# Down-projection of a gated MLP on one core: where the sums of weight quarters are made, how many raw tiles the ring holds, and beside which up-projection pairs the steps stand

## The chip, the core and the metric

The program runs on one core of a Trainium2 chip. The metric is the device time of one execution in microseconds (us), taken as the median of several. A core has TensorE (PE; its weight loads are listed as PEld), VectorE (DVE), ScalarE (ACT), GpSimd (POOL) and SyncE (SP, which here only issues transfers). They run beside each other and wait for each other by semaphores; 16 DMA engines move data between HBM and the core's SBUF. The clock that TensorE is granted has two levels, 1.2 and 2.4 GHz; the profile gives it as a share of the full one.

## The reference, cut to what matters

One layer of a hybrid decoder for 512 tokens of width 1024. Two token mixers come first (some 60% of the time, untouched). The change is in the conv-gated MLP and in the gated input embedding behind it:

```python
h = rms_norm(x, ffn_norm[i])
act, lin = jnp.split(h @ w_ffn_up[i], 2, axis=-1)            # 1024 -> 2 x 2816
act = causal_dwconv(act, w_ffn_conv[i]) + b_ffn_conv[i]
x = x + (jax.nn.gelu(act) * lin) @ w_ffn_down[i]             # 2816 -> 1024
g = jax.nn.sigmoid(rms_norm(x, ple_norm[i]) @ w_ple_gate[i])
x = x + g * (p[i] @ w_ple_proj[i])
return rms_norm(x, final_norm)
```

## The kernel before

Every product is made of three matmuls on float32r parts (high times high, high times low, low times high). A weight block is loaded as it is into a raw tile of a ring in SBUF (tag `raw`; in this part of the program four tiles of 8 KB per partition). `wsplit` then makes the high part on ScalarE (`whi`, L164) and the low part on VectorE (`wlo`, L165), 128x1024 numbers at a time; there are four buffers of each. A raw tile comes free when its last `wlo` is made, and only then can the transfer for the tile that takes its place start.

`up(j)`, j from 0 to 10, makes one pair of hidden blocks: 4 column blocks of 24 matmuls each (lines L169 to L171, output `pa`), then the convolution, the GELU and the product, on ScalarE and VectorE, into a tile `g2`. `combine` (L293 to L302) makes from each such tile the operands `ch` and `cl` of the down-projection.

The down-projection is a block algorithm of seven steps in place of eight products (`strassen`, table `STEPS`). It runs in three quarters called 1 to 3 here (`down(0)`, `down(1)`, `down(2)`): the first two have four row blocks (`kh` 4, 24 matmuls in a step), the last three (18 matmuls). Lines L333 to L335 are its matmuls, with the PSUM banks `sX`, `sZ` and `sY`; L1070 adds a finished bank to the residual x2. Each step needs one weight tile, which is a quarter of the block (1 MB; 0.75 MB in the last), or the sum of two, three or four quarters: step 0 "11", step 1 "11"+"12", step 2 "11"+"12"+"22", step 3 "22", step 4 "21", step 5 "12"+"22", step 6 all four. The sums are made by transfers: the first quarter is loaded from SP's queue, and each further one is added to what lies in the tile by an accumulating transfer that GpSimd issues, each of them after the one before has landed:

```python
if i == 0:
    nc.sync.dma_start(raw, blk)
else:
    nc.gpsimd.dma_start(raw, blk, accum_op=ALU.add)
```

Pairs and steps alternate: three steps behind pair 4, three behind pair 5 and one behind pair 6, and the same behind pairs 8, 9 and 10; quarter 3 runs its seven steps without a pair between. `over(q)` then combines the pairs that were ready before their quarter had its turn. In quarter 3, `add` also starts the norm of each token tile that is complete (`x3n0` to `x3n3`: square on ScalarE, a small chain on GpSimd, scaling on VectorE, transposes on TensorE into h3). Two products follow: p with w_ple_proj (`pb` with operand pTh, in two halves of 24 matmuls) and h3 with w_ple_gate (`pb` with operand h3h).

The instructions of an engine run in the order in which the program lists them. That order, and the slots of tiles, were set by a scheduler when the program was built; `with ahead()` puts weight loads and splits as early as their buffers allow.

Of the kernel before, what the change touches and what calls it, by code (L numbers as in the profile page):

```python
# [14 lines left out]
P = 128  # L15
# [28 lines left out]
def tile_hybrid_block(  # L44
# [244 lines left out]
    def combine(pool, g2, ch, cl, j):  # L289
# [14 lines left out]
            op0=ALU.mult, op1=ALU.subtract,  # L304
        )

    def strassen(src, ch, cl, kh, add):

        v = src.rearrange("(k two p) n -> two p k n", two=2, p=P)
        banks = {}
        for n, (c, parts, b, th, h, sign) in enumerate(STEPS):
            with ahead():
                raw = rp[0].tile([P, kh, 512], F32, tag="raw", name=f"raw{uid()}", bufs=rp[1])
                for i, q in enumerate(parts):
                    blk = v[int(q[0]) - 1][:, :, 512 * int(q[1]) - 512 : 512 * int(q[1])]
                    if i == 0:
                        nc.sync.dma_start(raw, blk)
                    else:  # L320
                        nc.gpsimd.dma_start(raw, blk, accum_op=ALU.add)  # L321
                ws = [wsplit(raw[:, k : min(k + 2, kh), :], min(2, kh - k), 512) for k in range(0, kh, 2)]
            new = b not in banks
            if new:
                banks[b] = [sm_ps(f"s{b}{uid()}") for _ in range(2)]
            for t in range(2):
                ps = banks[b][t]
                tok = slice(t * P, (t + 1) * P)
                for k in range(kh):
                    hi, lo = ws[k // 2]  # L330
                    a_h, a_l = ch[:, c, k, tok], cl[:, c, k, tok]

                    TE.matmul(ps, lhsT=a_h, rhs=hi[:, k % 2, :], start=new and k == 0, stop=False, skip_group_check=True)  # L333
# [10 lines left out]
    class Norm:  # L344


        def __init__(self, pool, xt, name, tag="xn", bufs=4):
            self.x = [xt[:, :512], xt[:, 512:]]
            self.name = name
            self.xn = [pool.tile([P, 512], F32, tag=tag, name=f"{name}_{h}", bufs=bufs) for h in range(2)]  # L350
            self.ss = cp.tile([P, 4], F32, tag="ss", name=name + "s", bufs=4)
            self.rs = cp.tile([P, 1], F32, tag="rs", name=name + "r", bufs=4)
            self.n = 0
# [69 lines left out]
    with tc.tile_pool(name="xin", bufs=1, reuse_waits="tile") as xin:  # L423
        with ahead(200000):
            xts = [xin.tile([P, D], F32, name=f"xt{t}") for t in range(NT)]
            raw0 = [rp[0].tile([P, KD, 2 * P], F32, tag="raw", name=f"raw0_{i}", bufs=rp[1]) for i in range(2)]

            def load_x(t):
                nc.sync.dma_start(xts[t], x[t * P : (t + 1) * P, :])

            def load_w(i):
                nc.sync.dma_start(
                    raw0[i // 2][:, :, i % 2 * P : (i % 2 + 1) * P], srcs0[i].rearrange("(k p) n -> p k n", p=P)
                )

            load_x(0)
            g1 = gain_bc(xin, "g1", mixer_norm)
            load_x(1)
            load_w(0)
            load_x(2)  # L440
            load_w(1)
            load_x(3)
            load_w(2)
            load_w(3)
            nms = [Norm(xin, xts[t], f"xn{t}") for t in range(NT)]

            def sq(t):
                nms[t].square(0)
                nms[t].gather()
                nms[t].square(1, eng=V if t < 2 else None)  # L450

            def w0(i, eng=V):
                return wsplit(raw0[i // 2][:, :, i % 2 * P : (i % 2 + 1) * P], KD, P, eng=eng)

            sq(0)
            sq(1)
            norm_T(nms[0], g1, hT, 0)
            ws0 = [w0(0, G)]
            norm_T(nms[1], g1, hT, 1)
            for t in (2, 3):  # L460
                sq(t)
                ws0.append(w0(t - 1))
                for h in range(2):
                    nms[t].gained(g1, h)
                nms[t].rstd()
                for h in range(2):
                    transpose_split(nms[t].scaled_gained(h, V), hT, t, h, nms[t].name + "T")
            ws0.append(w0(3))
# [523 lines left out]
    for t in range(NT):  # L992
        nc.scalar.dma_start(x2[t], x[t * P : (t + 1) * P, :])
    lnp = ctx.enter_context(tc.tile_pool(name="lnp", bufs=1, side="right", reuse_waits="tile"))
    g2 = gain_bc(lnp, "g2", ffn_norm)
    h2 = new_hT("h2")

    def residual(nm, h, after=None):
        cols = slice(h * 512, (h + 1) * 512)

        def emit(t, ps):
            V.tensor_tensor(x2[t][:, cols], x2[t][:, cols], ps, op=ALU.add)
            if h == 1:
# [16 lines left out]

    rx.close()
    fx = ExitStack()
    rp[:] = fx.enter_context(tc.tile_pool(name="rp2", bufs=1, reuse_waits="tile")), 4
    fax = ExitStack()
    cmp = fax.enter_context(tc.tile_pool(name="cmp", bufs=1, reuse_waits="tile"))
    ch = cmp.tile([P, 7, 4, 256], R, name="ch")
# [37 lines left out]
    def down(q):  # L1064
        kh = min(4, KF // 2 - 4 * q)
        last = 4 * q + kh == KF // 2

        def add(t, h, ps, sign, n):
            xs = x2[t][:, h * 512 : (h + 1) * 512]
            V.tensor_tensor(xs, xs, ps, op=ALU.add if sign > 0 else ALU.subtract)  # L1070
            if not last:
                return

            if n in (3, 5):
                nms[t] = Norm(lnp, x2[t], f"x3n{t}")
                nms[t].square(1)
                nms[t].gather()
            elif n in (4, 6):
                nms[t].square(0)
                norm_T(nms[t], g3, h3, t)  # L1080

        return strassen(w_ffn_down[1024 * q : 1024 * q + 256 * kh, :], ch, cl, kh, add)
# [13 lines left out]
    for j in range(4):  # L1096
        up(j)
    d = down(0)
    for j, n in ((4, 3), (5, 3), (6, 1)):
        up(j)  # L1100
        run(d, n)
    over(0)
    up(7)
    g3 = gain_bc(lnp, "g3", ple_norm)
    d = down(1)
    for j, n in ((8, 3), (9, 3), (10, 1)):
        up(j)
        run(d, n)
    over(1)
    h3 = new_hT("h3")  # L1110

    def quad(name, dt=F32):
        return cmp.tile([P, 2, T], dt, tag="g2", name=name, bufs=5)


    pt = quad("pt").rearrange("p a (t d) -> p (a t) d", t=2)
    nc.sync.dma_start(pt, p.rearrange("(t q) d -> q t d", q=P))
    pTh, pTl = quad("pTh", R), quad("pTl", R)
    for k in range(2):
        ps = sm_ps(f"pT{k}")  # L1120
        for t in range(NT):
            TE.transpose(ps[:, t * P : (t + 1) * P], pt[:, t, k * P : (k + 1) * P], ident)
        S.copy(pTh[:, k, :], ps)
        V.tensor_tensor(pTl[:, k, :], ps, f32(pTh[:, k, :]), op=ALU.subtract)
    run(down(2), 7)

    pjs = [rp[0].tile([P, 4, 512], F32, tag="raw", name=f"pj{i}", bufs=rp[1]) for i in range(2)]
    pj = [[pjs[t // 2][:, 2 * (t % 2) + h, :] for h in range(2)] for t in range(NT)]
    for h in range(2):
        cols = slice(h * 512, (h + 1) * 512)  # L1130
        proj_b(w_ple_proj[:, cols], (pTh, pTl), 2, lambda t, ps: S.copy(pj[t][h], ps))
    fax.close()
    gtp = fx.enter_context(tc.tile_pool(name="gtp", bufs=1, reuse_waits="tile"))

# [6 lines left out]
    def add_gated(t, h, a, b, ps):  # L1141
        s = piece(f"psig{h}_{t}_{a}")[:, a:b]
        xs = x2[t][:, 512 * h + a : 512 * h + b]
        S.activation(s, ps, AF.Sigmoid)
        V.tensor_tensor(s, s, pj[t][h][:, a:b], op=ALU.mult)
        V.tensor_tensor(xs, xs, s, op=ALU.add)
        if h == 0:
            fin[t] = Norm(gtp, x2[t], f"on{t}", "g", 24)
        fin[t].square(h, a, b)
        if (h, b) != (1, 512):  # L1150
            fin[t].gather()
        if h == 0:
# [70 lines left out]
```

## Time and profile before

| | us |
|---|---|
| median of 3 runs | 1210.12 (1208.36 to 1212.64) |
| the profiled execution | 1207.67 |
| its span, from the first to the last instruction | 1205.9 |
| mean granted TensorE clock over the span | 0.988 |

The span is the trace's own length; the execution is 1.77 us longer. Times of rows count from the start of the span. A matmul's duration in a row is modelled and overlaps the next one's, so the pace of TensorE is read from the distance of starts. In a timeline row the bracket gives the engine's idle time just ahead of it and what ended that.

### The profile page before, as it was taken

The numbers are of one execution on the slowest core, as the hardware profiler recorded it, in microseconds if no ns is written. First come the engines' busy times: TensorE is split into PE (matmuls) and PEld (weight loads), VectorE is DVE, ScalarE is ACT, GpSimd is POOL, SyncE is SP. The second block draws the span as 40 slices with busy tenths as digits, with TensorE's granted clock in tenths as the row PEclk, the third lists the DMA queues.
The fourth block names the chain that finished last, engine by engine and source line by source line (L and its number), as shares of the span: only waits on it lengthen the run. The fifth ranks groups of instructions, "written<-read, shape, count | busy, mean of one in ns | idle before, by whom it ended". The sixth has DMA issues, their size and how long they took to land.

```text
span 1205.9 us, 14072 instructions
## 1 busy us (share of the span) xinstructions
PE 1161.5 (96%) x5540; PEld 958.6 (79%) x5540; DVE 665.8 (55%) x864; ACT 518.7 (43%) x850; POOL 160.6 (13%) x178
## 2 busy tenths in 40 slices
PE   6999999999999999999999999999999999988696
PEld 6887887888887778888888888988888788866485
DVE  5867657676667356342333344665556556537455
ACT  4666483662572155443432322544343343424443
POOL 7004023040031000000111000000000010012202
PEclk9999999999999999999999999999999999989898
DMA  7332123222231253223143335434776696698431
GB/s 204 105 105 71 35 71 95 80 71 70 73 91 47 70 175 105 71 70 101 46 115 82 94 105 140 119 109 123 161 205 167 148 214 178 155 203 193 103 123 70
DMA packets 160370, 137.59 MB, mean 114 GB/s; under 512 B 5792, under 2 KB 125216, under 8 KB 160304
## 3 DMA queue, kind: packets, MB, share of 16 engines
q1 hardware_dynamic: 149536, 114.41, 32.4%
q0 software_dynamic: 10192, 20.19, 9.7%
q10 hardware_dynamic: 576, 2.10, 0.5%
q8 instruction: 43, 0.70, 0.2%
q14 instruction: 23, 0.19, 0.0%
HBM read 134.58 MB, written 2.10 MB: 113 GB/s over the span
## 4 chain that ended last, share of the span: by engine, by line
PE 84%; DMA 6%; DVE 4%; issue 2%; ACT 2%; POOL 1%; SPq 1%; POOLq 0%; ACTq 0%; DVEq 0%
PE pa L170 16%; PE pa L169 16%; PE pa L171 16%; PE pb L249 7%; PE pb L251 7%; PE pb L250 7%; DMA raw<-in_w_ffn_down_dram 5%; PE yd L608 2%; PE sX L333 1%; PE sX L334 1%; PE sX L335 1%; PE st L616 1%; DVE wlo L165 1%; PE yo L605 1%; DMA raw<-in_w_in_dram 1%
## 5 line engine op out<-in xcount | busy, mean ns | idle before, releaser
L165 DVE TENSOR_TENSOR wlo<-raw,whi 128x1024 fp32r<-128x1024 f32 x208 | 255.6, 1234 | 305.3 <-ACT whi L164 305.0
L164 ACT CAST whi<-raw 128x1024 fp32r<-128x1024 f32 (+2 forms) x209 | 216.1, 1039 | 390.6 <-PE pa L170 205.3
L169 PE MATMUL pa<-h1h,whi 128*128 128x512 f32 (+1 forms) x416 | 159.4, 383 | 0.2 <-ACT h1h L403 0.2
L171 PE MATMUL pa<-h1h,wlo 128*128 128x512 f32 (+1 forms) x416 | 157.3, 378 | 0.0
L170 PE MATMUL pa<-h1l,whi 128*128 128x512 f32 (+1 forms) x416 | 156.6, 377 | 0.1
L169 PE MATMUL pa<-h2h,whi 128*128 128x512 f32 (+1 forms) x384 | 142.7, 372 | 0.0
L170 PE MATMUL pa<-h2l,whi 128*128 128x512 f32 (+1 forms) x384 | 142.6, 372 | 0.0
L171 PE MATMUL pa<-h2h,wlo 128*128 128x512 f32 (+1 forms) x384 | 142.6, 372 | 0.0
L249 PE MATMUL pb<-whi,h1h 128*128 128x512 f32 x256 | 99.7, 394 | 0.8 <-DVE accb L668 0.8
L250 PE MATMUL pb<-wlo,h1h 128*128 128x512 f32 x256 | 99.8, 390 | 0.0
L251 PE MATMUL pb<-whi,h1l 128*128 128x512 f32 x256 | 99.4, 392 | 0.0
L169 PEld LDWEIGHTS pa<-h1h,whi 128*128 128x128 f32 x416 | 79.2, 190 | 14.9 <-issue 0.7
L170 PEld LDWEIGHTS pa<-h1l,whi 128*128 128x128 f32 x416 | 79.1, 190 | 14.4 <-issue 0.7
L171 PEld LDWEIGHTS pa<-h1h,wlo 128*128 128x128 f32 x416 | 79.0, 190 | 13.9 <-issue 0.2
L171 PEld LDWEIGHTS pa<-h2h,wlo 128*128 128x128 f32 x384 | 72.4, 188 | 12.5
L169 PEld LDWEIGHTS pa<-h2h,whi 128*128 128x128 f32 x384 | 72.3, 188 | 12.5
L170 PEld LDWEIGHTS pa<-h2l,whi 128*128 128x128 f32 x384 | 72.4, 188 | 12.4
L321 POOL DMA_DIRECT2D raw<-in_w_ffn_down_dram x21 | 27.2, 1373 | 330.0 <-DVE wlo L165 184.6
L249 PEld LDWEIGHTS pb<-whi,h1h 128*128 128x128 f32 x256 | 48.1, 188 | 10.5 <-DVE accb L668 1.2
L251 PEld LDWEIGHTS pb<-whi,h1l 128*128 128x128 f32 x256 | 48.1, 188 | 9.8
L250 PEld LDWEIGHTS pb<-wlo,h1h 128*128 128x128 f32 x256 | 48.1, 188 | 9.3
L533 DVE SCALAR_TENSOR_TENSOR acc<-pa,prm,acc 128x511 f32<-128x511 f32 (+2 forms) x72 | 52.6, 742 | 2.9 <-ACT acc L531 2.0
(376 smaller groups left out, 2011.1 us busy)
## 6 DMA issues: line engine op xcount, KB each, us to landing
raw<-in_w_in_dram SPq DMA_DIRECT2D x48, 512.0 KB, 5.2
raw<-in_w_ffn_up_dram SPq DMA_DIRECT2D x44, 512.0 KB, 5.6
raw<-in_w_in_dram SPq DMA_DIRECT2D x16, 1024.0 KB, 5.0
raw<-in_w_ffn_down_dram SPq DMA_DIRECT2D x14, 1024.0 KB, 5.3
raw<-in_w_ffn_down_dram POOLq DMA_DIRECT2D x14, 1024.0 KB, 10.4
raw<-in_w_branch_b_dram SPq DMA_DIRECT2D x32, 256.0 KB, 4.1
raw<-in_w_ffn_down_dram SPq DMA_DIRECT2D x7, 768.0 KB, 5.2
raw<-in_w_ffn_down_dram POOLq DMA_DIRECT2D x7, 768.0 KB, 8.5
```

What stands on the lines that cost most here:

```text
L164: S.copy(hi, raw)
L165: eng.tensor_tensor(lo, raw, f32(hi), op=ALU.subtract)
L169: TE.matmul(ps, lhsT=lh, rhs=rh, start=first, stop=False)
L170: TE.matmul(ps, lhsT=lh, rhs=rl, start=False, stop=False)
L171: TE.matmul(ps, lhsT=ll, rhs=rh, start=False, stop=last)
L249: TE.matmul(pss[t], lhsT=a, rhs=hi[:, kk, :], start=first, stop=False)
L250: TE.matmul(pss[t], lhsT=a, rhs=lo[:, kk, :], start=False, stop=False)
L251: TE.matmul(pss[t], lhsT=b, rhs=hi[:, kk, :], start=False, stop=last)
L321: nc.gpsimd.dma_start(raw, blk, accum_op=ALU.add)
L333: TE.matmul(ps, lhsT=a_h, rhs=hi[:, k % 2, :], start=new and k == 0, stop=False, skip_group_check=True)
L533: V.scalar_tensor_tensor(out=acc[:, s:], in0=ps[:, : T - s], scalar=cw[:, ct, 3 - s : 4 - s], in1=acc[:, s:], op0=ALU.mult, op1=ALU.add,)
L608: TE.matmul(py[:, j * 64 : (j + 1) * 64], lhsT=L[:, j, :], rhs=xdt[:, j * 64 : (j + 1) * 64], start=True, stop=True,)
```

## The change

- Steps 0, 1, 3, 4 and 5 load as before (one or two quarters). Step 2 no longer has a tile: GpSimd adds the tile of "22" to that of "11"+"12" in place, 128x1024 numbers at a time, and step 6 adds the tile of "21" on top of it. Both are tiles that steps 3 and 4 use anyway.
- The ring has five raw tiles in place of four. To make room the norms' scratch tiles moved, with their numbers of buffers (first norm: pool `xnp`, two buffers of 2x512; the norms behind the down-projection: the buffers of tag `g2`; the last norm: tag `on`).
- Four steps stand behind pair 4 and three behind pair 5, and then pairs 6 and 7; the same with pairs 8 and 9. Pair 10 and the first half of the product with w_ple_proj stand between quarters 2 and 3; that half stays in PSUM (`held`) until quarter 3 is done.

```diff
+    def weights(r, v, parts, kh):
+        n = len(parts)
+        if n < 3:
+            raw = r[parts] = rp[0].tile([P, kh, 512], F32, tag="raw", name=f"raw{uid()}", bufs=rp[1])
+            for i, q in enumerate(parts):
+                blk = v[int(q[0]) - 1][:, :, 512 * int(q[1]) - 512 : 512 * int(q[1])]
+                if i == 0:
+                    nc.sync.dma_start(raw, blk)
+                else:
+                    nc.gpsimd.dma_start(raw, blk, accum_op=ALU.add)
+            return raw
+        raw, more = (r["11", "12"], "22") if n == 3 else (r["11", "12"], "21")
+        if (more,) not in r:
+            weights(r, v, (more,), kh)
+        for k in range(0, kh, 2):
+            q = slice(k, min(k + 2, kh))
+            G.tensor_tensor(raw[:, q, :], raw[:, q, :], r[more,][:, q, :], op=ALU.add)
+        return raw
...
             with ahead():
-                raw = rp[0].tile([P, kh, 512], F32, tag="raw", name=f"raw{uid()}", bufs=rp[1])
-                for i, q in enumerate(parts):
...
+                raw = r[parts] if parts in r else weights(r, v, parts, kh)
...
-    rp[:] = fx.enter_context(tc.tile_pool(name="rp2", bufs=1, reuse_waits="tile")), 4
+    rp[:] = fx.enter_context(tc.tile_pool(name="rp2", bufs=1, reuse_waits="tile")), 5
...
-                nms[t] = Norm(lnp, x2[t], f"x3n{t}")
+                nms[t] = Norm(cmp, x2[t], f"x3n{t}", "g2", 5)
...
-    for j, n in ((4, 3), (5, 3), (6, 1)):
+    for j, n in ((4, 4), (5, 3)):
         up(j)
         run(d, n)
     over(0)
+    up(6)
     up(7)
     g3 = gain_bc(lnp, "g3", ple_norm)
     d = down(1)
-    for j, n in ((8, 3), (9, 3), (10, 1)):
+    for j, n in ((8, 4), (9, 3)):
         up(j)
         run(d, n)
     over(1)
...
+    up(10)
+    h3 = new_hT("h3")
+
+    held = []
+    proj_b(w_ple_proj[:, :512], (pTh, pTl), 2, lambda t, ps: held.append(ps))
     run(down(2), 7)
...
-    for h in range(2):
-        cols = slice(h * 512, (h + 1) * 512)
-        proj_b(w_ple_proj[:, cols], (pTh, pTl), 2, lambda t, ps: S.copy(pj[t][h], ps))
+    for t in range(NT):
+        S.copy(pj[t][0], held[t])
+    proj_b(w_ple_proj[:, 512:], (pTh, pTl), 2, lambda t, ps: S.copy(pj[t][1], ps))
```

GpSimd's own list from its first work for quarter 1 on, before and then after the change (in it raw_6542 and raw_6538 are the tiles of "11"+"12" in the one and the other program, raw_6581 that of step 2, raw_6826 that of step 5, raw_6996 that of step 6; in the new one raw_6577 is "22", raw_6782 "21" and raw_6820 the tile of step 5; rows from raw_7401 and raw_7392 on are those of quarter 2):

```order
L321 DMA raw_6542<-in_w_ffn_down_dram 128x4x512
L321 DMA raw_6581<-in_w_ffn_down_dram 128x4x512 x2
L321 DMA raw_6826<-in_w_ffn_down_dram 128x4x512
L321 DMA raw_6996<-in_w_ffn_down_dram 128x4x512 x3
L321 DMA raw_7401<-in_w_ffn_down_dram 128x4x512
```

```order
L318 DMA raw_6538<-in_w_ffn_down_dram 128x4x512
L325 TENSOR_TENSOR raw_6538<-raw_6538,raw_6577 128x1024 x2
L325 TENSOR_TENSOR raw_6538<-raw_6538,raw_6782 128x1024 x2
L318 DMA raw_6820<-in_w_ffn_down_dram 128x4x512
L318 DMA raw_7392<-in_w_ffn_down_dram 128x4x512
```

Seven accumulating transfers of a quarter have become two and four additions, and the transfer for step 5 now stands behind the additions for step 6.

TensorE's list where quarter 3 begins, before and then after (pT are the transposes of p, sX_7969 is step 0 of quarter 3, pa_7902 is the last block of pair 10, pb_7945 the first tile of the product with w_ple_proj):

```order
L333 MATMUL sX_7374<-whi_7864,ch 128x512
L334 MATMUL sX_7374<-wlo_7865,ch 128x512
L335 MATMUL sX_7374<-whi_7864,cl 128x512
L1122 MATMUL pT_7945<-ident,pt 128x128 x4
L1122 MATMUL pT_7952<-ident,pt 128x128 x4
L333 MATMUL sX_7969<-whi_7961,ch 128x512
```

```order
L171 MATMUL pa_7902<-h2h,wlo_7899 128x512
L169 MATMUL pa_7902<-h2h,whi_7898 128x512
L170 MATMUL pa_7902<-h2l,whi_7898 128x512
L171 MATMUL pa_7902<-h2h,wlo_7899 128x512
L249 MATMUL pb_7945<-whi_7951,pTh 128x512
L250 MATMUL pb_7945<-wlo_7952,pTh 128x512
```

Before, quarter 3 followed step 6 of quarter 2 and the transposes of p at once; now pair 10 and 18 of the 24 matmuls of the first product stand in between, and the transposes stand between steps 5 and 6 of quarter 2.

TensorE's list where the first norm's transposes stand in quarter 3, before and then after (sX_7970 and sX_7990 end step 5; sY_8109 is the second token tile of step 4; sX_7989 with whi_8227 begins step 6):

```order
L334 MATMUL sX_7970<-wlo_8176,ch 128x512
L335 MATMUL sX_7970<-whi_8175,cl 128x512
L401 MATMUL x3n0T_8124<-ident,x3n_0_8076 128x128 x4
L401 MATMUL x3n0T_8132<-ident,x3n_1_8077 128x128 x4
L333 MATMUL sY_8109<-whi_8100,ch 128x512
L334 MATMUL sY_8109<-wlo_8101,ch 128x512
```

```order
L349 MATMUL sX_7990<-wlo_8192,ch 128x512
L350 MATMUL sX_7990<-whi_8191,cl 128x512
L417 MATMUL x3n0T_8140<-ident,x3n_8094 128x128 x4
L417 MATMUL x3n0T_8148<-ident,x3n_8094 128x128 x4
L348 MATMUL sX_7989<-whi_8227,ch 128x512
L348 MATMUL sX_7990<-whi_8227,ch 128x512
L349 MATMUL sX_7989<-wlo_8228,ch 128x512
```

The second token tile of step 4 stood right behind the transposes; now step 6 does, and that tile (sY_8125) follows behind step 6.

## Rows read from the trace of the kernel before

**Rows 1.** The page: TensorE's busy time, and its granted clock in 40 slices.

```profile
PE 1161.5 (96%) x5540; PEld 958.6 (79%) x5540; DVE 665.8 (55%) x864; ACT 518.7 (43%) x850; POOL 160.6 (13%) x178
PEclk9999999999999999999999999999999999989898
```

**Rows 2.** Windows: a pair without waits, then quarters 1, 2, 3 and their pairs.

```profile
core 0: us, PE busy (x) PEld busy (x) DVE busy (x) ACT busy (x) POOL busy (x), PEclk, DMA share, GB/s
886.08:907.84 21.76, 21.76 (x97) 18.02 (x96) 10.07 (x11) 6.87 (x9) 1.28 (x1) 1.00 0.72 182
...
869.76:999.11 129.35, 127.09 (x554) 104.62 (x552) 75.93 (x104) 49.94 (x67) 8.97 (x7) 0.99 0.73 179
999.11:1087.72 88.61, 84.75 (x361) 69.21 (x360) 48.54 (x64) 30.91 (x39) 9.01 (x7) 0.96 0.73 178
1087.72:1151.44 63.72, 50.65 (x218) 38.91 (x217) 40.21 (x59) 29.76 (x56) 11.68 (x16) 0.92 0.67 156
```

**Rows 3.** TensorE's timeline: start, duration, instruction, and idle time before with its ender.

```profile
869.76 0.39 PE L333 MATMUL sX<-whi,ch 128*128 128x512 f32 x1
...
880.64 0.39 PE L333 MATMUL sX<-whi,ch 128*128 128x512 f32 x1
...
947.58 0.50 PE L333 MATMUL sX<-whi,ch 128*128 128x512 f32 x1 [1.50 <-ACT whi L164]
...
1078.83 0.80 PE L333 MATMUL sX<-whi,ch 128*128 128x512 f32 x1 [3.40 <-ACT whi L164]
...
1108.60 0.73 PE L333 MATMUL sX<-whi,ch 128*128 128x512 f32 x2 [1.53 <-ACT whi L164]
...
1116.34 1.32 PE L401 MATMUL x3n0T<-ident,x3n 128*128 128x128 f32 x8 [1.33 <-DVE x3n L378]
1118.80 0.56 PE L333 MATMUL sY<-whi,ch 128*128 128x512 f32 x1 [1.14 <-DVE h3l L404]
...
1128.86 1.22 PE L333 MATMUL sX<-whi,ch 128*128 128x512 f32 x2 [6.14 <-ACT whi L164]
...
1150.85 0.39 PE L249 MATMUL pb<-whi,h3h 128*128 128x512 f32 x1
```

**Rows 4.** The chain that ended last, around the waits of quarters 1 and 3.

```profile
916.22 10.94 DMA raw<-in_w_ffn_down_dram
...
928.72 8.30 issue
...
1103.31 9.09 DMA raw<-in_w_ffn_down_dram
...
1130.91 0.43 PE sX L335
```

**Rows 5.** Groups of instructions from 860 to 1160 us: VectorE's, then ScalarE's.

```profile
L165 DVE TENSOR_TENSOR wlo<-raw,whi 128x1024 fp32r<-128x1024 f32 x65 | 79.1, 1222 | 82.2 <-ACT whi L164 82.2
...
L164 ACT CAST whi<-raw 128x1024 fp32r<-128x1024 f32 x64 | 66.9, 1051 | 111.2 <-DMA raw<-in_w_ffn_down_dram 44.7 <-PE pa L170 38.0 <-PE sX L335 11.8
```

**Rows 6.** GpSimd's timeline: its one 128x1024 operation, and two of 128x512.

```profile
10.64 2.83 POOL L165 TENSOR_TENSOR wlo<-raw,whi 128x1024 fp32r<-128x1024 f32 x1 [0.85 <-ACT whi L164]
...
113.49 1.04 POOL L621 TENSOR_TENSOR S<-S,cdb 128x512 f32<-128x512 f32 x1
...
357.00 2.02 POOL L614 TENSOR_TENSOR xdc<-Xg,qt 128x512 f32<-128x512 f32 x1
```

**Rows 7.** Transfers issued between 800 and 1150 us: count, size, median to landing.

```profile
raw<-in_w_ffn_down_dram SPq DMA_DIRECT2D x14, 1024.0 KB, 5.3
raw<-in_w_ffn_down_dram POOLq DMA_DIRECT2D x14, 1024.0 KB, 10.4
```

**Rows 8.** VectorE's timeline at steps 0 and 1, then its durations on line L165.

```profile
859.94 1.23 DVE L165 TENSOR_TENSOR wlo<-raw,whi 128x1024 fp32r<-128x1024 f32 x1 [2.77 <-ACT whi L164]
...
871.03 1.22 DVE L165 TENSOR_TENSOR wlo<-raw,whi 128x1024 fp32r<-128x1024 f32 x1
...
L165 DVE TENSOR_TENSOR wlo<-raw,whi x208: 558/1225/2080, 13.7 to 1175.5; 128x1024 fp32r<-128x1024 f32 x104
```

More of the change, by code (lines that the diff above doesn't have):

```diff
@@ L305, in combine @@
         )
+    def weights(r, v, parts, kh):
[16 more added lines that the diff above has]
+        return raw
     def strassen(src, ch, cl, kh, add):
         v = src.rearrange("(k two p) n -> two p k n", two=2, p=P)
-        banks = {}
+        banks, r = {}, {}
         for n, (c, parts, b, th, h, sign) in enumerate(STEPS):
             with ahead():
-                raw = rp[0].tile([P, kh, 512], F32, tag="raw", name=f"raw{uid()}", bufs=rp[1])
-                for i, q in enumerate(parts):
[L317 to L321, printed above, removed]
+                raw = r[parts] if parts in r else weights(r, v, parts, kh)
                 ws = [wsplit(raw[:, k : min(k + 2, kh), :], min(2, kh - k), 512) for k in range(0, kh, 2)]
@@ L344, in tile_hybrid_block, with __init__ @@
     class Norm:
-        def __init__(self, pool, xt, name, tag="xn", bufs=4):
+        def __init__(self, pool, xt, name, tag="xn", bufs=2):
             self.x = [xt[:, :512], xt[:, 512:]]
             self.name = name
-            self.xn = [pool.tile([P, 512], F32, tag=tag, name=f"{name}_{h}", bufs=bufs) for h in range(2)]
+            xn = pool.tile([P, 2, 512], F32, tag=tag, name=name, bufs=bufs)
+            self.xn = [xn[:, h, :] for h in range(2)]
             self.ss = cp.tile([P, 4], F32, tag="ss", name=name + "s", bufs=4)
@@ L444, in tile_hybrid_block @@
             load_w(3)
-            nms = [Norm(xin, xts[t], f"xn{t}") for t in range(NT)]
+            nms = [Norm(xin, xts[t], f"xn{t}", bufs=4) for t in range(NT)]
             def sq(t):
@@ L994, in tile_hybrid_block @@
     lnp = ctx.enter_context(tc.tile_pool(name="lnp", bufs=1, side="right", reuse_waits="tile"))
+    xnp = gx.enter_context(tc.tile_pool(name="xnp", bufs=1, side="right", reuse_waits="tile"))
     g2 = gain_bc(lnp, "g2", ffn_norm)
@@ L1003, in emit @@
             if h == 1:
-                n = Norm(lnp, x2[t], f"{nm}{t}")
+                n = Norm(xnp, x2[t], f"{nm}{t}")
                 n.square(0)
@@ L1109, in tile_hybrid_block @@
     over(1)
[L1110 to L1116, printed above, removed]
+    pt = rp[0].tile([P, NT, 256], F32, tag="raw", name="pt", bufs=rp[1])
     nc.sync.dma_start(pt, p.rearrange("(t q) d -> q t d", q=P))
-    pTh, pTl = quad("pTh", R), quad("pTl", R)
+    pTh, pTl = (cmp.tile([P, 2, T], R, tag="g2", name=f"pT{c}", bufs=5) for c in "hl")
     for k in range(2):
@@ L1147, in add_gated @@
         if h == 0:
-            fin[t] = Norm(gtp, x2[t], f"on{t}", "g", 24)
+            fin[t] = Norm(gtp, x2[t], f"on{t}", "on", 4)
         fin[t].square(h, a, b)
```

## The prediction

> **What bounds the kernel now.** I read the page first. TensorE is busy 96% of the span and its clock is full up to slice 37 but for modelled ends [rows 1], so there is little to win outside the last quarter of the time; the reader should see that 44 us of the span (1205.9 less 1161.5) are without a matmul, and that some 11 of these lie behind the last matmul, where this change does nothing. Then I put a clean pace beside the stretch that the change touches. A pair of 96 matmuls without a wait took 21.76 us at a clock of 1.00: 0.2267 us each [rows 2]. With that the three quarters and their pairs can be priced:
>
> - quarter 1, from its first matmul to quarter 2's: 7 x 24 + 4 x 96 = 552 matmuls, 125.1 us at that pace, took 129.35: 4.2 lost;
> - quarter 2, to the transposes of p: 7 x 24 + 2 x 96 = 360 matmuls, 81.6 us, took 88.61: 7.0 lost;
> - quarter 3, to the first matmul with h3: 7 x 18 + 48 = 174 matmuls, 39.4 us, and 40 transposes at about 1.0 us for eight (an estimate from the eight of x3n0T, whose 1.32 us ends in a modelled end), 5.0 us. It took 63.1 us, from 1087.72 to 1150.85: 18.7 lost [rows 2, 3].
>
> Together 29.9 us. That is all that any change in this stretch can win, and the ceiling of mine. The loss has two parts, idle time and the slow matmuls behind it: the granted clock was 0.96 and 0.92 in quarters 2 and 3, and at 1130.91, behind the longest gap, matmuls were 0.43 us apart, that is at the lower of the two levels, 1.2 GHz [rows 2, 4].
>
> Third, TensorE's timeline for who ended each gap [rows 3]. Four gaps end with ScalarE's `whi`, a weight split that came late: 947.58 (1.50 us), 1078.83 (3.40), 1108.60 (1.53), 1128.86 (6.14). Two belong to the norm in quarter 3: 1.33 us ahead of the transposes x3n0T, and 1.14 behind them, where the second tile of step 4 waits for h3l. Fourth, the chain that ended last, for why the splits were late: it goes back through accumulating transfers, one behind the other, of 10.94 us at 916.22 and 9.09 us at 1103.31, and an "issue" piece of 8.30 us between them, in which GpSimd had issued the second of three and waited for it to land [rows 4]. Plain loads land after 5.3 us, accumulating ones after 10.4 [rows 7]: the tile of step 6 needs 5.3 + 3 x 10.4 = 36.5 us and a split of 2.3 from the moment that its slot is free. That slot is step 4's, split about 3 us before step 4 begins; until step 6's turn there are then 3 + 2 x 5.44 + 21.76 = 36 us. The 3 us that are missing are the gap at 947.58 and the slow start behind it.
>
> **The change, part by part.** *Transfers.* Per quarter, seven plain and seven accumulating transfers become five and two. What goes is 3 x 5 = 15 accumulating transfers and six loads; only those on the chain count, and they are steps 5 and 6 of every quarter. Steps 1 and 5 keep one accumulation each.
>
> *Additions.* Twelve come, four in each quarter, eight of 128x1024 and in quarter 3 two of those and two of 128x512. The trace has no such addition. Its nearest row is GpSimd's one two-input operation of 128x1024, 2.83 us, which I take; the bounds are twice the shortest and the longest of 128x512, 2.1 and 4.0 us [rows 6]. Do they stand on the path? Up to 869.76 both programs have the same matmuls in the same order, so I can use this trace's times. Step 1's two halves are split by 866.8 and 872.25 (the second from the row at 871.03) [rows 8]. The additions for step 2 start behind each: done at 869.6 and 875.1. Step 2's second half then needs a cast of 1.05 and a subtraction of 1.22 [rows 5] and is ready at 877.4, with an addition to x2 ahead of it some 0.7 later. TensorE starts step 2 at 880.64 [rows 3] and needs that half six matmuls later, at 882.0. With 4.0 us instead of 2.83 it is ready at 879.3. Cost: nothing, hidden behind step 1's matmuls; without that cover each addition would cost its 2.83. The condition for a stall follows from the same sum: two additions in a row from 866.8 on, and 2.3 us of split, reach 882.0 when one addition takes 6.5 us.
>
> *What is queued behind them.* "21" takes the slot of step 0's tile, free at 861.2 [rows 8], and is there at 866.5; its additions run after step 2's splits, by about 883; step 6 needs them at 924. Step 5's accumulation now stands behind these in GpSimd's list. Its own load waits for the slot of "22", free at about 883 when step 3 is split: 883 + 5.3 + 10.4 = 899, needed at 919. Twenty us to spare. Quarter 2 repeats this.
>
> *Five slots and the moved steps.* Each up-projection load starts one tile, half a pair or 10.9 us, earlier. SP's list loses the two tiles of steps 2 and 6, so no load stands longer behind another's wait; the transfer of p and the loads of quarter 3 stand behind pair 10's and wait only for slots that pair 10's and the projection's splits free. For quarter 3 the last of these is step 5's: the projection's weights can be split when pair 10's first block is done, 16.3 us before the pair ends; load and accumulation end at about that pair's end, 24 us before step 5. The combination of pair 10 now has the projection's first 18 matmuls, 4.1 us, as its cover; before, three combinations stood between quarters 2 and 3 with the transposes alone. It also costs: in quarters 1 and 2 step 6 now follows step 5 at once and must wait for VectorE's additions of that bank (0.7 us), while two combinations run. By their order a block of the next pair stands between the two token tiles, so I put this at 0, and at 1 us for each quarter without that cover.
>
> *What stays in quarter 3.* The norm of the first token tile takes 5 us from sY's last matmul to its transposes and has only step 5, 4.1 us, beside it, so a gap of about 1 us stays. Behind it step 6's split stands on VectorE after the norm's two scalings and two additions to x2, some 1.5 us late. I keep 2.5 us of gaps there, and 2 us for slow matmuls behind them and for the other three norms, which now have the second half of the projection and 17 matmuls with h3 in front of their transposes: 4.5 us in all, bounds 0 and 9 (9 is what quarter 3 loses now without the gaps at 1108.60 and 1128.86 and the slow matmuls behind the second).
>
> *Sum.* 29.9 - 4.5 = 25.4 us. The profiled execution, 1207.67, becomes 1182.3; the median of the runs shown lies 2.45 above that execution, so 1184.7, rounded to 1185.
>
> **A rule that speaks against the change.** The row shows 2.83 us for the shape on GpSimd, against VectorE's 1.22 [rows 5, 6], and the same kind of operation between 1.04 and 2.02 us for half the size. The Trainium skill, page "GPSIMD Engine Reference", section 3 "Performance versus the Vector engine", says that ordinary elementwise work belongs on VectorE, which is about twice as fast; its 4497 ns for 2048 numbers would make the addition 2.25 us (an estimate from that page), inside my bounds, and the sum the same. Section 8 "Key points" of that page says that GpSimd shares its SBUF interfaces with VectorE and collides with instructions that have two SBUF inputs. Every `wlo` is one. That is the second rival.
>
> **The rivals.**
>
> 1. *All of it* (6%): no gap stays. 1210.1 - 29.9 = 1180.
> 2. *Additions and splits slow each other* (22%). For: the durations of `wlo` reach 2.08 us against a median of 1.23 [rows 8], and GpSimd's spread is twofold [rows 6]. Against: the sum above with both at their longest, 872.25 + 4.0 + 1.05 + 2.08 = 879.4, still meets 882.0. If other work on VectorE takes those 2.6 us too, step 2 of each quarter waits about as the gap at 947.58 did, which cost quarter 1 its 4.2 us: 3 x 4.2 = 12.6, gain 12.8, time 1197.
> 3. *The waits stay as large, no change* (4%). The steps' tiles would have to come as late as now by another way, such as step 5's transfer behind the additions: it needs a delay of 20 us that I cannot find.
> 4. *Slower* (5%): the additions are the new bound. Above 6.5 us for one, step 2 waits twice the excess. With slow matmuls behind a gap doubling its price, all 25 us are gone at a wait of 4.2 us in each quarter, that is at about 8.6 us for an addition, and at 10 us (a wait of 7.1, doubled, three times) the time is some 1227. Against it: that is over three times the row.
>
> That the change doesn't do what it says is excluded by GpSimd's list: the additions stand there and the transfers are gone.
>
> **How the numbers follow.** The forecast has 63%: 1181 to 1190, from 4.5 lost with its bounds 0 and 9, and 1185 as its middle. Rival 2 reaches to 1199, rival 1 below to 1178 with the 2 us by which runs differ. The range 1178 to 1199 leaves out rivals 3 and 4 and little more. Faster by over 0.3% (3.6 us, about what a measurement of this kernel can tell from no change) has 91% (rivals 1 and 2 and the forecast), within it 4%, slower 5%.
>
> **What would show it.** Right: no gap on TensorE that ends with `whi` in quarters 1 and 2; windows of the same matmuls at 125 and 82 us and a clock of 1.00; additions of 2 to 4 us; a gap of about 1 us ahead of x3n0T as the largest of quarter 3. Wrong: gaps ended by GpSimd's additions ahead of step 2 (rivals 2 and 4), or an accumulating transfer still in the chain that ended last.

## The result, and the profile after

The changed kernel takes 1178.81 us, the median of 4 runs (1175.74 to 1180.49), where the kernel before, run beside it, takes 1211.38 (1208.36 to 1215.54, 4 runs): ratio 0.9726, with a 95% interval from 0.9688 to 0.9764. The profiled execution is the slowest of the four, 1180.49 us with a span of 1178.5; that of before was 1207.67 with 1205.9. Between these two the gain is 27.2 us, between the medians 32.6.

The page's lines for TensorE, to set beside [rows 1]:

```profile
PE 1157.1 (98%) x5540; PEld 957.9 (81%) x5540; DVE 677.4 (57%) x864; ACT 520.5 (44%) x850; POOL 171.1 (15%) x175
PEclk9998999999999999999999999999999999999999
```

TensorE is without a matmul for 21.4 us of the span where it was 44.4. The slices of a lower clock at the end are gone; one in the fourth slice is new, in a part that the change doesn't touch (the last section comes back to it).

Windows of the changed kernel: quarter 1 with its pairs, quarter 2 with its pairs and pair 10, the first product's first 18 matmuls and quarter 3 up to the first matmul with h3, and the gate product. They answer to [rows 2].

```profile
core 0: us, PE busy (x) PEld busy (x) DVE busy (x) ACT busy (x) POOL busy (x), PEclk, DMA share, GB/s
874.39:999.51 125.12, 125.12 (x553) 103.60 (x552) 81.20 (x104) 50.99 (x67) 12.28 (x6) 1.00 0.47 126
999.51:1082.01 82.50, 82.50 (x370) 68.40 (x368) 56.28 (x68) 33.53 (x43) 11.13 (x6) 1.00 0.53 131
1082.01:1124.41 42.40, 41.67 (x183) 33.34 (x182) 34.59 (x44) 25.44 (x46) 14.76 (x16) 1.00 0.29 92
1124.41:1171.13 46.72, 46.72 (x241) 39.72 (x239) 28.22 (x36) 21.58 (x40) 11.19 (x16) 1.00 0.14 52
```

At 0.2267 us for a matmul the first window is 552 of them and nothing else (125.1), the second 360 (81.6) and eight transposes (0.9); the third has 174 matmuls (39.4) and eight transposes (1.3), which leaves 1.7. The clock is 1.00 throughout.

TensorE's timeline at these borders, with every gap above 0.25 us from 874.39 on, to set beside [rows 3]:

```profile
874.39 0.39 PE L348 MATMUL sX<-whi,ch 128*128 128x512 f32 x1
...
999.51 0.39 PE L348 MATMUL sX<-whi,ch 128*128 128x512 f32 x1
...
1110.20 1.26 PE L417 MATMUL x3n0T<-ident,x3n 128*128 128x128 f32 x8
...
1113.13 0.50 PE L349 MATMUL sX<-wlo,ch 128*128 128x512 f32 x1 [0.64 <-DVE wlo L165]
...
1124.41 0.39 PE L249 MATMUL pb<-whi,h3h 128*128 128x512 f32 x1
...
1170.85 0.28 PE L268 MATMUL pb<-whi,h3l 128*128 128x256 f32 x1
```

Of the gaps of [rows 3] none is left; the only one is 0.64 us inside step 6. From the first matmul of quarter 1 to the end of the last matmul of the program it was 325.1 us (869.76 to 1194.84) and is 296.7 (874.39 to 1171.13): 28.3 us saved. Behind the last matmul it was 11.1 us and is 7.4: 3.7 more, which I had not forecast. Ahead of quarter 1 the profiled execution is 4.6 us later than that of before. 28.3 + 3.7 - 4.6 = 27.4, the difference of the spans.

GpSimd's timeline in quarter 1, for the additions:

```profile
871.53 2.38 POOL L325 TENSOR_TENSOR raw<-raw,raw 128x1024 f32<-128x1024 f32 x1 [41.54 <-DVE wlo L165]
876.96 2.52 POOL L325 TENSOR_TENSOR raw<-raw,raw 128x1024 f32<-128x1024 f32 x1 [3.05 <-DVE wlo L165]
881.12 2.40 POOL L325 TENSOR_TENSOR raw<-raw,raw 128x1024 f32<-128x1024 f32 x1 [1.65 <-DVE wlo L165]
884.68 2.41 POOL L325 TENSOR_TENSOR raw<-raw,raw 128x1024 f32<-128x1024 f32 x1 [1.16 <-DVE wlo L165]
896.09 1.29 POOL L318 DMA_DIRECT2D raw<-in_w_ffn_down_dram  x1 [9.00 <-issue]
```

The ten of 128x1024 take 2.47 us in the mean, the two of 128x512 in quarter 3 take 1.29.

### The profile page after: what moved, and what is told of

The parts are those of the page before. It is cut to its first block, busy times and chain, and to the rows that moved or that the text cites. A ratio compares the mean times of both kernels' runs of the same rounds, so it can differ in the third digit from the quotient of the medians.

```text
span 1178.5 us, 14049 instructions
## 1 busy us (share of the span) xinstructions
PE 1157.1 (98%) x5540; PEld 957.9 (81%) x5540; DVE 677.4 (57%) x864; ACT 520.5 (44%) x850; POOL 171.1 (15%) x175
## 4 chain that ended last, share of the span: by engine, by line
PE 96%; DVE 1%; DMA 1%; SPq 1%; POOL 1%; issue 0%; ACT 0%; POOLq 0%; ACTq 0%
PE pa L170 18%; PE pa L169 18%; PE pa L171 17%; PE pb L249 8%; PE pb L251 8%; PE pb L250 8%; PE yd L624 3%; PE sX L348 2%; PE sX L349 2%; PE sX L350 2%; PE st L632 1%; PE yo L621 1%; PE sZ L348 1%; PE sZ L349 1%; PE sZ L350 1%; DMA raw<-in_w_in_dram 1%
## 5 line engine op out<-in xcount | busy, mean ns | idle before, releaser
L165 DVE TENSOR_TENSOR wlo<-raw,whi 128x1024 fp32r<-128x1024 f32 (+1 forms) x208 | 261.5, 1263 | 255.2 <-ACT whi L164 255.0
L164 ACT CAST whi<-raw 128x1024 fp32r<-128x1024 f32 (+1 forms) x209 | 216.9, 1039 | 359.5 <-PE pa L170 219.2
L170 PE MATMUL pa<-obl,whi 128*128 128x512 f32 x128 | 51.9, 406 | 0.0
```

The lines of the kernel that those rows point to most:

```text
L164: S.copy(hi, raw)
L165: eng.tensor_tensor(lo, raw, f32(hi), op=ALU.subtract)
L170: TE.matmul(ps, lhsT=lh, rhs=rl, start=False, stop=False)
```

## Experiments: which of the three parts

The change has three parts: the additions on GpSimd, the ring of five, and the order of pairs and steps. Six kernels, all made from the changed one, hold one or two of them, so that with the kernel before and the changed kernel every combination has a time. (The norms' scratch stays in its new place in all six; in the kernel before it is in its old one.)

**e1, transfer sums again.**

```diff
-        if n < 3:
+        if n < 5:
             raw = r[parts] = rp[0].tile([P, kh, 512], F32, tag="raw", name=f"raw{uid()}", bufs=rp[1])
```

> The changed kernel, but the sums of three and four quarters are made by accumulating transfers again; ring of five and new order stay. Theory A (the chain of transfers behind one another made the splits late, and the additions on GpSimd cure that): step 6's tile needs 36.5 us of transfers and 2.3 of split; with five slots its slot is free about 41 us ahead of step 6 in quarters 1 and 2, so these lose 0 to 2 us each, but in quarter 3, where the steps follow each other at 4.1 us, it comes 2 to 8 us late, with slow matmuls behind the gap: 1183 to 1192. Rival B (five slots and the new order do it all, whoever makes the sums): within 2 us of the changed kernel, 1177 to 1181.

**e2, ring of four.**

```diff
-    rp[:] = fx.enter_context(tc.tile_pool(name="rp2", bufs=1, reuse_waits="tile")), 5
+    rp[:] = fx.enter_context(tc.tile_pool(name="rp2", bufs=1, reuse_waits="tile")), 4
```

> The changed kernel with a ring of four raw tiles; additions on GpSimd and new order stay. Theory A: loads start half a pair later, but no chain is longer than one load and one accumulation; quarters 1 and 2 lose 0 to 3 us each, quarter 3 some 3 us at step 5, whose tile waits for the slot of the tile of 22: 1181 to 1188. Rival B (the slots do it): 12 us or more come back, 1191 to 1210.

**e3, old order.**

```diff
-    for j, n in ((4, 4), (5, 3)):
+    for j, n in ((4, 3), (5, 3), (6, 1)):
...
-    up(6)
     up(7)
...
-    for j, n in ((8, 4), (9, 3)):
+    for j, n in ((8, 3), (9, 3), (10, 1)):
...
-    up(10)
...
-    proj_b(w_ple_proj[:, :512], (pTh, pTl), 2, lambda t, ps: held.append(ps))
     run(down(2), 7)
...
+    for h in range(2):
+        proj_b(w_ple_proj[:, h * 512 : (h + 1) * 512], (pTh, pTl), 2, lambda t, ps: S.copy(pj[t][h], ps))
```

> The changed kernel with the steps beside the pairs where they stood before, and pair 10 and the projection's first half not ahead of quarter 3; additions on GpSimd and the ring of five stay. Theory A: quarters 1 and 2 lose nothing; quarter 3 loses 1 to 3 us more around the norms and the combinations; and if the order of the gate's matmuls behind quarter 3 set the shorter tail, up to 3.7 us of that come back: 1179 to 1187. Rival C (the moved steps are the larger part of the gain): 1192 to 1210.

**e4, order alone** (the edits of e1 and e2 together).

> Only the new order (and the norms' scratch in its new place): sums by accumulating transfers and a ring of four, as before. Theory A: the late splits stay, step 6's slot is free 36 us ahead for a need of 39, as before, and in quarter 3 it is 6 us or more late; only the shorter tail and what the combinations and norms cost is won: 1199 to 1211. Rival C (the order is the larger part): 1178 to 1194.

**e5, sums alone** (the edits of e2 and e3).

> Only the additions on GpSimd (and the norms' scratch in its new place): a ring of four and the old order, as before. Theory A: nearly the whole gain of the changed kernel, less what its order gives in quarter 3 and behind the last matmul (e3 lay some 4 us above it): 1180 to 1187. Rival D (additions need the fifth slot or the new order, since two tiles stay held while pair 6 or 10 runs): 1192 to 1205.

**e6, ring alone** (the edits of e1 and e3).

> Only the ring of five (and the scratch): sums by accumulating transfers, the old order. Theory A: in quarters 1 and 2 the fifth slot gives step 6's chain one tile, 5.4 us, of lead for the 3 us that were missing, so these gaps close; in quarter 3 it gives 4.1 us of 6 to 8, so a part stays: 1193 to 1201. Rival: the tile of step 6 is set by GpSimd's queue of transfers and not by its slot, so that a fifth slot brings nothing: 1206 to 1213.

Measured; "stretch" is from the first matmul of quarter 1 to the end of the last matmul, "behind" is the rest of the span, both in the profiled execution:

| | sums | slots | order | median us | ratio to before (95%) | stretch | behind |
|---|---|---|---|---|---|---|---|
| before | transfers | 4 | old | | 1 | 325.1 | 11.1 |
| e4 | transfers | 4 | new | 1208.85 | 0.9970 (0.9945 to 0.9995) | 325.7 | 7.9 |
| e6 | transfers | 5 | old | 1193.20 | 0.9832 (0.9780 to 0.9884) | 314.7 | 7.9 |
| e1 | transfers | 5 | new | 1193.96 | 0.9858 (0.9821 to 0.9895) | 309.6 | 7.5 |
| e5 | GpSimd | 4 | old | 1176.68 | 0.9697 (0.9655 to 0.9739) | 297.8 | 7.4 |
| e3 | GpSimd | 5 | old | 1182.94 | 0.9758 (0.9730 to 0.9786) | 298.7 | 7.4 |
| e2 | GpSimd | 4 | new | 1178.61 | 0.9739 (0.9706 to 0.9772) | 297.2 | 7.4 |
| changed | GpSimd | 5 | new | 1178.81 | 0.9726 (0.9688 to 0.9764) | 296.7 | 7.4 |

The additions alone bring the whole gain of the stretch. Once they are there, the fifth slot and the new order are worth 1 us of the stretch together (297.8 against 296.7), and the intervals overlap. The order alone brings nothing in the stretch. The ring alone closes the gaps of quarters 1 and 2, as the working in the prediction had it (3 us missing, one step of 5.4 us more), and leaves quarter 3. e2 and e5 came out below what I expected of them: the 3 us that I gave to step 5 of quarter 3 with four slots were not lost, and step 6's gap of 0.63 us is again the only one there in e2. e1 came out above: quarter 1 takes 2.6 us more than in the changed kernel, where I had expected 0 to 2, and quarter 3 takes 9.9 more, where I had expected 2 to 8. Its timeline of TensorE and, for quarter 3, the chain that ended last show why:

```profile
934.55 0.47 PE L348 MATMUL sX<-whi,ch 128*128 128x512 f32 x1 [2.35 <-DVE x L1087]
...
1121.12 1.97 PE L417 MATMUL x3n0T<-ident,x3n 128*128 128x128 f32 x8 [4.65 <-DVE x3n L394]
...
1126.15 1.22 PE L348 MATMUL sX<-whi,ch 128*128 128x512 f32 x2 [3.07 <-ACT whi L164]
```

```profile
1102.08 7.33 DMA raw<-in_w_ffn_down_dram
...
1109.69 7.49 DMA raw<-in_w_ffn_down_dram
...
1117.47 7.49 DMA raw<-in_w_ffn_down_dram
1125.06 1.05 ACT whi L164
1126.15 1.22 PE sX L348 x2
```

The gap of 2.35 us is step 6 of quarter 1, whose bank VectorE frees (L1087) only behind step 6's own late low parts. In quarter 3 three transfers of some 7.4 us, each issued when the one before has landed, end in step 6's split. And the first norm is late too: its small steps stand in GpSimd's list behind the issue of the third transfer, which itself waits until 1117.47. GpSimd's timeline of e1 at that place:

```profile
1117.47 1.26 POOL L318 DMA_DIRECT2D raw<-in_w_ffn_down_dram  x1 [6.51 <-DMA raw<-in_w_ffn_down_dram]
1118.81 0.19 POOL L384 TENSOR_SCALAR x3n0s<-x3n0s 128x1 f32<-128x1 f32 x1
```

In e6 the two gaps of quarter 3 are 8.95 and 2.87 us. A chain of transfers on GpSimd thus delays not only its own tile but whatever GpSimd does next.

## Experiments: what the additions cost

**e8 and e9, longer additions.** The edit of e8, and below it that of e9:

```diff
-            G.tensor_tensor(raw[:, q, :], raw[:, q, :], r[more,][:, q, :], op=ALU.add)
+            for o in range(3): G.tensor_tensor(raw[:, q, :], raw[:, q, :], r[more,][:, q, :], op=ALU.subtract if o % 2 else ALU.add)
```

```diff
+            for o, z in ((ALU.add, q), (ALU.subtract, slice(k, k + 1)), (ALU.add, slice(k, k + 1))): G.tensor_tensor(raw[:, z, :], raw[:, z, :], r[more,][:, z, :], op=o)
```

> The changed kernel with each of the twelve additions made three times (add, subtract, add; the sum is the same but for rounding), 7.4 us in place of 2.5. Theory A with its condition of 6.5 us: step 2's second half comes some 2 us late in quarters 1 and 2, up to twice that with slow matmuls behind it, and in quarter 3 step 6's additions and the norm's small steps behind them on GpSimd come 1 to 4 us late: 1183 to 1191. Rival (the additions have far more room than that): within 2 us of the changed kernel. Rival (they have no room at all): 12 additions x 4.9 us = 59 us, some 1238.

> The changed kernel, each addition followed by a subtraction and an addition of the same numbers over half of it, so that one takes about 2.5 + 1.3 + 1.3 = 5 us. By the prediction's condition (a stall above 6.5 us) nothing is lost: within 2 us of the changed kernel, 1176 to 1182. By what the tripled additions showed (VectorE's splits beside a GpSimd that adds without a pause took 3.1 us in place of 1.2), step 2's second split is ready at about 887 against a need of 886.6: up to 2 us lost in each quarter, twice with slow matmuls behind: 1181 to 1190.

e8 took 1201.28 us (ratio 0.9914, 0.9882 to 0.9946), stretch 322.6: 25.9 us longer than in the changed kernel, far more than expected. e9 took 1186.16 (0.9797, 0.9767 to 0.9826), stretch 306.5: 9.8 longer, where the condition of 6.5 us had nothing lost and the second reading had 1181 to 1190. GpSimd's timeline of e8 in quarter 1, and then VectorE's beside it:

```profile
871.44 7.40 POOL L325 TENSOR_TENSOR raw<-raw,raw 128x1024 f32<-128x1024 f32 x3 [41.96 <-DVE wlo L165]
880.00 5.05 POOL L325 TENSOR_TENSOR raw<-raw,raw 128x1024 f32<-128x1024 f32 x2 [1.16 <-DVE wlo L165]
886.22 17.37 POOL L325 TENSOR_TENSOR raw<-raw,raw 128x1024 f32<-128x1024 f32 x6 [1.16 <-DVE wlo L165]
```

```profile
876.50 3.42 DVE L165 TENSOR_TENSOR wlo<-raw,whi 128x1024 fp32r<-128x1024 f32 x1
879.85 0.41 DVE L294 TENSOR_TENSOR cmb<-cmb,g 128x256 f32<-128x256 f32 x1
880.18 0.67 DVE L1087 TENSOR_TENSOR x<-x,sX 128x512 f32<-128x512 f32 x1
...
883.32 2.82 DVE L165 TENSOR_TENSOR wlo<-raw,whi 128x1024 fp32r<-128x1024 f32 x1
...
886.66 2.25 DVE L300 TENSOR_TENSOR cl<-cmb,ch 128x256 fp32r<-128x256 f32 x1
...
892.22 12.45 DVE L165 TENSOR_TENSOR wlo<-raw,whi 128x1024 fp32r<-128x1024 f32 x4 [0.83 <-ACT whi L164]
```

A low part, 1.22 us by itself, takes 2.3 to 3.4 beside an addition in these runs. The rows show a wait and not a slower pace: the one begun at 876.50 ends 1.08 us behind the addition beside it (at 879.92; the addition ends at 871.44 + 7.40 = 878.84), the one begun at 883.32 ends 1.09 behind its own (886.14 and 885.05), though the first had 2.3 us beside the addition and the second 1.7. Nearly all of its work thus comes behind the addition's end, and a short instruction is stretched by more: `cl` on 128x256 numbers takes 2.25 us, where `cmb` on as many takes 0.41 when begun between two additions. GpSimd waits in its turn. Its 30 additions of 128x1024 take 2.67 us in the mean, against 2.47 in the changed kernel, but the three from 893.69 to 903.58, beside low parts without a pause, take 3.23, 3.35 and 3.27. The addition to x2, whose second input lies in PSUM, keeps its 0.67. The first gap of e9, in TensorE's timeline, the low part that ends it, in VectorE's, and GpSimd's additions of quarter 1 (three instructions for each of four):

```profile
887.93 0.50 PE L349 MATMUL sZ<-wlo,ch 128*128 128x512 f32 x1 [1.41 <-DVE wlo L165]
```

```profile
884.46 3.41 DVE L165 TENSOR_TENSOR wlo<-raw,whi 128x1024 fp32r<-128x1024 f32 x1
```

```profile
866.95 5.36 POOL L325 TENSOR_TENSOR raw<-raw,raw 128x1024 f32<-128x1024 f32 x3 [41.69 <-DVE wlo L165]
873.47 19.21 POOL L325 TENSOR_TENSOR raw<-raw,raw 128x1024 f32<-128x1024 f32 x9 [1.16 <-DVE wlo L165]
```

In quarters 1 and 2 of e9 it is step 3 that waits, not step 2: its tile needs no sum, but its low part stands beside the additions for step 6. In e8 it is step 2, the one that the condition speaks of: its gaps in quarter 1 add up to 4.2 us (0.39, 3.48 and 0.34). Behind the longest the matmuls are 0.43 us apart from 895.34 to 899.61, TensorE's lower level of 1.2 GHz, and the quarter takes 133.6 us, 8.5 more than in the changed kernel.

**e11, no additions**: the loop with the addition is taken out, so that steps 2 and 6 multiply by the sum of two quarters. **e10, additions on VectorE.** **e12**, the changed kernel again, on the same chip.

```diff
-            G.tensor_tensor(raw[:, q, :], raw[:, q, :], r[more,][:, q, :], op=ALU.add)
+            V.tensor_tensor(raw[:, q, :], raw[:, q, :], r[more,][:, q, :], op=ALU.add)
```

> The changed kernel without its twelve additions: steps 2 and 6 multiply by the sum of the first two quarters, so that the sums of three and four are left out. Theory A (the additions are hidden): within 1.5 us of the changed kernel, 1175 to 1181; only the gap of 0.6 us ahead of step 6 in quarter 3 may go. Rival (additions and splits slow each other on the path): 3 to 6 us faster, 1171 to 1175.

> The changed kernel with its twelve additions on VectorE in place of GpSimd, in the same order of TensorE. They take about 1.2 us each, 14 us more on an engine that is busy 65 and 68% in quarters 1 and 2 and 82% in quarter 3. Theory A (what counts is that no transfer chain stands behind; the additions are hidden on either engine): within 2 us of the changed kernel, 1176 to 1182, and no split beside them longer than 2.1 us. Rival (VectorE is full in quarter 3, and its additions push step 6's split and the norms): 2 to 5 us slower than the changed kernel, 1181 to 1187.

> The changed kernel once more, for a comparison on the same chip as these three: 1175 to 1181, ratio to before about 0.972, as before; e5, with the additions alone, stood at 0.9697.

e11: 1180.94 us, 0.9734 (0.9705 to 0.9763), stretch 296.7. e10: 1177.31, 0.9721 (0.9691 to 0.9751), stretch 296.8. e12: 1180.20, 0.9726 (0.9694 to 0.9758), stretch 296.7. Three times the same: the additions cost the path nothing, on GpSimd or on VectorE, and the gap of 0.64 us inside step 6 has nothing to do with them. VectorE's group of low parts in e10 and then in the changed kernel, both from 860 to 1160 us:

```profile
L165 DVE TENSOR_TENSOR wlo<-raw,whi 128x1024 fp32r<-128x1024 f32 x68 | 84.0, 1242 | 38.1 <-ACT whi L164 38.1
L325 DVE TENSOR_TENSOR raw<-raw,raw 128x1024 f32<-128x1024 f32 x10 | 12.2, 1220 | 0.1
```

```profile
L165 DVE TENSOR_TENSOR wlo<-raw,whi 128x1024 fp32r<-128x1024 f32 x69 | 89.9, 1309 | 39.1 <-ACT whi L164 39.0
```

In the changed kernel the additions cost VectorE some 5 us of longer low parts (69 of 1309 ns against 1242); on VectorE itself they cost it 13.6 us. Neither is on the path.

## Experiment: what lies behind the last matmul

**e7, gate product by token tiles**, in the kernel before:

```diff
-            lambda t, ps, a=0, b=512: add_gated(t, h, a, b, ps), tail=h == 1, split_last=h == 1,
+            lambda t, ps, a=0, b=512: add_gated(t, h, a, b, ps), tail=True, split_last=h == 1,
```

> The kernel before with one thing changed: the first half of the product with w_ple_gate goes token tile by token tile instead of row block by row block. Theory T (in the kernel before the four tiles end together, their sigmoids and norms pile up on ScalarE and VectorE, and the pile lasts to the end): the stretch behind the last matmul shrinks from 11.1 to about 7.4 us, time 3 to 4 us under before, ratio about 0.997. Rival (the tail is set by the last token tile alone): within 1 us of before, ratio 0.999 to 1.001.

1208.47 us, 0.9955 (0.9928 to 0.9981). Behind the last matmul it takes 8.0 us in place of 11.1; the stretch ahead is 1.2 longer (326.3), so that the two profiled executions differ by 2.0. What fills ScalarE there, in the kernel before and then in the changed one (psig is the sigmoid of a gate tile, on the square for the last norm):

```profile
1169.73 0.60 ACT L1144 ACTIVATE psig<-pb 128x512 f32<-128x512 f32 x1
1171.88 0.63 ACT L363 ACTIVATE on<-x 128x512 f32<-128x512 f32 x1 [1.54 <-DVE x L1146]
...
1172.51 0.58 ACT L1144 ACTIVATE psig<-pb 128x512 f32<-128x512 f32 x1
...
1175.63 0.63 ACT L363 ACTIVATE on<-x 128x512 f32<-128x512 f32 x1 [1.60 <-DVE x L1146]
...
1176.26 0.58 ACT L1144 ACTIVATE psig<-pb 128x512 f32<-128x512 f32 x1
```

```profile
1137.12 0.60 ACT L1162 ACTIVATE psig<-pb 128x512 f32<-128x512 f32 x1
1139.27 0.63 ACT L379 ACTIVATE on<-x 128x512 f32<-128x512 f32 x1 [1.55 <-DVE x L1164]
...
1146.38 0.60 ACT L1162 ACTIVATE psig<-pb 128x512 f32<-128x512 f32 x1 [0.26 <-PE pb L251]
1147.74 0.60 ACT L1162 ACTIVATE psig<-pb 128x512 f32<-128x512 f32 x1 [0.76 <-PE pb L251]
```

Before, ScalarE's list has each tile's square ahead of the next tile's sigmoid, so that the tiles go through ScalarE and VectorE one after the other, 3.75 us each, from 25 us before TensorE's end on, and ScalarE and VectorE finish behind it. In the changed kernel the first tile is done early, two sigmoids follow each other, and the later sigmoids wait only for their own matmuls. That the spread of these tiles sets the tail is shown by e7. The early first tile is not needed for it: in e3, e5 and e6 the first sigmoid starts 25.1 us before TensorE's end, as in the kernel before, but the second starts 24.6 before it and not 22.3, and the tail is 7.4 to 7.9. Which edit of the change made ScalarE's order another is not shown: e4 to e6 have a tail of 7.4 to 7.9 with either order of steps and either kind of sums, so what they share, the moved scratch of the norms, is the candidate; it was not tried alone.

## Why the prediction held, point by point

- **The number.** 1178.81 lies in the range of 1178 to 1199, but below the 1181 to 1190 of the forecast itself, and beside the 1180 of rival 1, which had no gap left and 6%. Two terms, told below, make the difference: less stayed in quarter 3 (1.6 us, not 4.5), and 3.7 us went behind the last matmul, which no term held. Without these 3.7 the time would be some 1182.5; with them it is in the range by 0.8 us, and that is luck.
- **The loss and its cause.** Quarter 1's 4.2 us and quarter 2's 7.0 came back whole. That the chain of accumulating transfers was the cause is shown: with it, every kernel loses at least 12 us against the same one without it (309.6 against 296.7 with five slots and the new order, 325.7 against 297.2 with four).
- **The additions hidden behind step 1.** They start 0.1 us behind the time worked out (866.8 and 872.25 become 871.4 and 876.9 with the 4.6 us of this execution; measured 871.53 and 876.96), last 2.47 us in the mean where I took 2.83, and e11 puts their cost at 0.0.
- **What is queued behind them.** Those for step 6 end at 887.1 (forecast 883, shifted 887.6); step 5's accumulation follows at 896.09, and nothing waits for it.
- **The 4.5 us kept in quarter 3** were mis-sized: 29.9 - 28.3 = 1.6 us stayed. The gap of about 1 us ahead of x3n0T is not there, since the norm's first half is ready at 1110.08, 3.5 us behind sY's last matmul (1106.6) and not 5, and TensorE is at step 5 until 1110.20; the 1.5 us ahead of step 6 are 0.64; no slow matmuls stand behind them (clock 1.00). Why the norm takes less is not shown.
- **"Some 11 of these lie behind the last matmul, where this change does nothing"** was wrong: 3.7 us of them went. This and the 1.6 kept are why the gain exceeds 25.4: 25.4 + 2.9 + 3.7 = 32.0 of which the profiled execution gave 4.6 back ahead of quarter 1. The medians, which hold other executions, differ by 32.6.
- **The slots and the moved steps.** I described what they do and gave them no term of their own; e2, e4 and e5 say that they have none in this kernel beside the additions. No rival gave the gain to them, though: without the additions the fifth slot alone takes 10.4 us off the stretch (e6, 325.1 to 314.7).
- **Rival 2, additions and splits slow each other**, is real as a mechanism and had no price here. The changed kernel's VectorE shows it at the second pair of additions, where a low part lasts 3.04 us and ends 1.07 behind the addition of 881.12 (2.40 us):

```profile
879.82 1.23 DVE L165 TENSOR_TENSOR wlo<-raw,whi 128x1024 fp32r<-128x1024 f32 x1
880.96 0.68 DVE L1087 TENSOR_TENSOR x<-x,sX 128x512 f32<-128x512 f32 x1
881.55 3.04 DVE L165 TENSOR_TENSOR wlo<-raw,whi 128x1024 fp32r<-128x1024 f32 x1
884.52 0.68 DVE L1087 TENSOR_TENSOR x<-x,sZ 128x512 f32<-128x512 f32 x1
```

  The Trainium skill, page "GPSIMD Engine Reference", section 8 "Key points", names VectorE's instructions with two SBUF inputs among those that collide with GpSimd; the rows agree, and those with one input in PSUM stay at 0.68. The Trainium skill, the same page, section 3 "Performance versus the Vector engine", has elementwise work belong on VectorE; this kernel does not decide it, since e10 and e12 agree within their intervals.
- **The condition of 6.5 us for a stall**, at which rival 4 begins, was wrong. It followed step 2's split alone, at VectorE's undisturbed pace. In e9 an addition, subtraction and addition last 5.36 us the first time and 6.4 in the mean of the other three (19.21 / 3), all that under 6.5, and step 2 is indeed in time in quarters 1 and 2; but step 3 waits there, through VectorE. So the room is smaller, and how far below 5.4 us it ends was not tried. At 8.0 us (three of 2.67) the loss is 25.9 us, near the 8.6 us at which rival 4 had the gain gone, and in quarter 1 in the way it had it: 4.2 us of gaps cost 8.5.
- **A slip in the first reading.** The clock is not full up to slice 37: the first slice below 90% in [rows 1] is the 36th (1055 to 1085 us), with the gap at 1078.83 in it. No term rests on it.

## What to carry to other kernels

A sum made by transfers that accumulate one behind the other is a serial chain on the issuing engine's list: count its length from the slot's release to the first use, and what else stands on that list. Either give it lead (a slot more) or do away with it; when an engine with room can add tiles that are loaded anyway, the slot is no longer needed. Before work is put on GpSimd, count for every VectorE instruction with two SBUF inputs that it may end only behind the GpSimd instruction beside it, also where that serves another step; and count what a change does to the work behind the last matmul, even when no edit touches it.

## What the runs showed of the hardware that was not expected

- GpSimd's additions of two SBUF tiles and VectorE's instructions with two SBUF inputs take turns: a low part of 1.22 us, begun beside an addition, ends 1.07 to 1.09 us behind the addition's end (three rows above), so that it takes up to 3.4 us; beside low parts without a pause, additions of 2.47 us in the mean take 3.2 to 3.4.
- One and the same wait of TensorE is followed by the lower clock in one execution and not in another. The changed kernel and e2 have the same order of TensorE up to quarter 1, and in both TensorE waits 1.58 us for VectorE just ahead of 109.3 us. Windows there, of the changed kernel and then of e2, with the granted clock as third number from the end:

```profile
80.00:120.00 40.00, 37.70 (x179) 29.79 (x178) 24.21 (x28) 25.35 (x56) 11.71 (x8) 0.89 0.33 102
```

```profile
80.00:120.00 40.00, 37.69 (x195) 30.48 (x194) 25.58 (x29) 25.39 (x56) 12.06 (x9) 1.00 0.34 102
```

  The 0.89 is a mean: from 111 to 121 us the changed kernel's clock is 0.50, the lower level. It reaches quarter 1 at 874.39, e2 at 869.90. What decides it is open. The four executions of e5 lie as far apart: 1176.65, 1176.67, 1176.70 and, with a lower clock in the same place in its profile, 1181.60 us. In e10 the clock falls at 402 us instead, in e1 and e4 at both places (at 111 and again at 408 in e1). A stretch counted from a common instruction is therefore a better measure than the span where 5 us matter.
